# Hybrid attention and recurrence step: transposes of the decayed keys inside the value projection, four sample pages a run in both stages

## The chip, the cores and the metric

The kernel runs on one core of one Trainium2 chip, in one launch. The metric is device time in microseconds (us). TensorE (PE) does the matmuls, VectorE (DVE), ScalarE (ACT) and GpSimd (POOL) the elementwise work. SyncE (SP) issues almost all DMAs, in the order of its queue.

## The reference, cut to what matters

One decoder layer with width 2048, on 512 prompt tokens and 8 sample sequences of 8 tokens (576 columns together). All results are float32.

```python
z = rms_norm(x) @ w_in            # one combined projection, split into the parts below
# eight heads: sparse attention, top-k keys by an indexer; the samples read paged keys and values
att = sparse_attend(q, k_sel, v_sel, valid)
# four heads: gated linear attention (keys 128 wide, values 256 wide), in chunks
cum   = cumsum(log_a)
decay = exp(where(causal, cum_t - cum_s, -inf))
o     = (q * exp(cum)) @ S + einsum('tk,sk,tsk->ts', q, k, decay) @ v
S_new = exp(cum_last) * S + (k * exp(cum_last - cum)).T @ v
# output: gate both groups, join them, multiply by w_out, add x, normalise
```

The product `k * exp(cum_last - cum)` is the decayed key, `kD` in the kernel. `S_new` sums over tokens, so the kernel needs `kD` with tokens on the partitions: that is what the transposes of `kD` give.

## The kernel before

**Numbers.** Every large product is made of three matmuls on split operands (high times high, low weights times high, high times low). A weight tile is loaded by `wload`: SP brings 128x512 floats (256 KB) into `w_raw` (three slots), ACT casts the high part (`w_hi`, L181, five slots), DVE, or POOL late in the kernel, subtracts the low part (`w_lo`, L183, five slots). `gemm`/`kmm` is a projection with the tokens as columns: 288 columns a matmul, two for each product (L219, into `ps_g`). `vgroup` projects 512 columns of values with the tokens on partitions: sixteen steps of k, each with four row tiles of three matmuls (L608 to L610) and one tile for the samples with two (L604, L605, into `ps_v`), 512 columns each, one weight tile a step. At its end it scales the rows into `v_tok` (L638) and `v_smp` (L644) and stores them to a buffer in memory (`sv`, L640, L648).

**Stages.** Heads 0 to 3 of the attention come first, with the indexer; then heads 4 to 7; then, from about 640 us, the four heads h=0 to 3 of the recurrence; from about 1046 us the output projection (L1205 to L1210).

**Sample attention** is written once, in the generator `unit`, and is drawn step by step into the other work by `fill`: after each half of a `gemm` and each second step of a `vgroup` a rate is added to a sum, and each time the sum reaches one the next step of the unit is issued. A unit reads sixteen pages of keys or values (`kt`, `vt`; 1 MB each, four DMAs of 256 KB, `page_dma` L157, issued behind the page that was three earlier) into a ring tagged `kv`, and multiplies them in runs. `run` issues the first matmul of a list (L252) and ties the rest behind it at high priority (L255), so that nothing comes between. The scores go into `pS` (which L755 starts with a bias), then softmax, transposes (L787, L790), and the products with `vt` into `pOs`; ACT scales these into `ob` (L820), four transposes bring them into `pt` (L823), DVE gates them (L826). The units of the attention's second stage have four pages a run and a ring of five. Those of the recurrence's stage have two pages a run and a ring of four: sixteen runs.

**The recurrence, head by head.** `project` makes the log decay first (`log_decay`: two small matmuls into `ps_z` L896, ACT L897, L899 and L900 with a table load each, DVE L901 and the scan L903 into `cum`) and then the two projections of queries (`qT`, L923) and keys (`kT`). `decays` forms `ev_ec` (ACT L936) and `qE`; POOL writes the differences for `kD` (L943, L944), ACT takes the exponential (L945), POOL multiplies by the keys (L946). TensorE transposes `kD` (four times L949, once L953), ACT and DVE make `kDt`, `kDs` and `ks` of it (L951 to L963). Then eight levels of the triangular product within a chunk are set up (POOL L981 and L982, ACT L983, DVE L984 and L985, into `lv_d`) and multiplied in two runs (`pl`). A `yield` stands at the start of each of the two, and in the main loop the caller draws `decays` on from inside the value projection (h=0 and 1), the projections of head 3 (h=2) or the gates (h=3; L912 and L915). `recur` loads the values back (`vtok` L1049, `vSg` L1050) and does the chunks (L1066, L1067, L1072), the samples (L1082, L1095) and the transposes of the result (L1110, L1113 into `oT`, by ACT L1111 and L1114).

**Order.** A scheduler fixes each engine's order when the kernel is built, from the order of the code and from priorities; weights and runs have a higher priority (`WOFF`). On the chip each engine works its own list strictly in that order.

Of the kernel before, what the change touches and what calls it, by code (L numbers as in the profile page):

```python
# [20 lines left out]
P = 128  # L21
# [98 lines left out]
def build(tc, I, O):  # L120
# [4 lines left out]
    R0, R1, RF = 0.42, 0.65, 1.1  # L125
# [469 lines left out]
    def vgroup(g, step):  # L595
# [17 lines left out]
        for k in range(NK):  # L613
            w.append(wload(I["wv"][g, :, k : k + 1, :]))
            xs = ev.tile([P, P], F32R, name="xs", tag="xs", bufs=4)
            with tc.high_priority(offset=WOFF):
                po_.tensor_copy(xs[:, :TS], xh[k][:, TP:].bitcast(F32))
                po_.tensor_copy(xs[:, TS:], xl[k][:, TP:].bitcast(F32))
            xs2.append(xs)
            if k == 1:  # L620
                for i in (0, 1, 4, 2, 3):
                    for kk in (0, 1):
                        mms(i, kk)
            elif k == NK - 1:
                for i in range(5):
                    for kk in (NK - 2, NK - 1):
                        mms(i, kk)
            elif 1 < k < NK - 2:
                for i in range(5):
                    mms(i, k)  # L630
            if k % 2:
                fill()
            if k % 4 == 3:
                step(k // 4)
# [75 lines left out]
    def head(h, bg, n):  # L710
# [7 lines left out]
        if h == 0:  # L718
            for f in (head_q, head_k):
                qk1.append(f(1))  # L720
                pump(bg, n)
            vgroup(0, lambda q4: pump(bg, 2))
            filler[0] = None
            for _ in first:
                pass
            pa_s.close()
            px["p"], px["s"] = pool("pd1", 1)
            pump(bg, 3)
        Pi = head_scores(h, q, k)
        if h == 4:  # L730
            vgroup(1, lambda q4: None)
# [10 lines left out]
    def unit(un, w, hg, span):  # L742
# [10 lines left out]
        for half in range(2):  # L753
            S = pm.tile([P, 512], F32, name="pS", tag="pu", bufs=1)
            pe.matmul(S, lsel[half], biasS[:, :512], start=True, stop=False)  # L755
            for b0 in range(0, 4, span):
                mms = []
                for bb in range(b0, b0 + span):
                    kt = un.tile([P, 4, 512], F32, name="kt", tag="kv", bufs=max(span + 1, 4))
# [34 lines left out]
        for j0 in range(0, NPAGE, span):  # L794
            mms = []
            for j in range(j0, j0 + span):
                vt = un.tile([P, 4, 512], F32, name="vt", tag="kv", bufs=max(span + 1, 4))
# [34 lines left out]
    def chain(*gens):  # L832
        for g in gens:
            yield from g
# [15 lines left out]
    us = chain(unit(un, 0, 0, 4), unit(un, 1, 0, 4))  # L850
# [11 lines left out]
    us = chain(unit(un, 0, 1, 2), unit(un, 1, 1, 2))  # L862
# [67 lines left out]
    def decays(h, qT, kT, cum):  # L930
# [16 lines left out]
        pt = mm1("pt")  # L947
        for i in range(4):
            pe.transpose(pt[:, P * i : P * (i + 1)], kD[:, P * i : P * (i + 1)], ident)  # L949
        kDt = gl.tile([P, 4, P], F32, name="kDt")  # L950
        se.copy(kDt, pt.rearrange("p (i d) -> p i d", i=4))  # L951
        pt = mm1("pt")
        pe.transpose(pt[:, :P], kD[:, T - P : T], ident)  # L953
        kDs = ev.tile([TS, P], F32, name="kDs", tag="e1", bufs=2)
        se.copy(kDs, pt[TS:, :P])
        ks = [gl.tile([96, P], F32R, name=f"ks{w}") for w in range(2)]
        kept[h] = eL, qE, kDt, ks
        for w in range(2):
            r = slice(32 * w, 32 * w + 32)
            lo_r, hi_r = ((32, 0), (0, 32))[w]  # L960
            se.copy(ks[w][hi_r : hi_r + 32], kDs[r])
            se.copy(ks[w][64:96], kDs[r])
            ve.tensor_tensor(out=ks[w][lo_r : lo_r + 32], in0=kDs[r], in1=ks[w][r].bitcast(F32), op=ALU.subtract)  # L963
        Qd = bass.AP(tensor=Qb.tensor, offset=Qb.offset, ap=[Qb.ap[0], [64, 4], [32 + DT, 2], [1, DT]])
        po_.tensor_copy(Qd, qE[:, TP:T].rearrange("p (m e t) -> p m e t", e=2, t=DT))

# [5 lines left out]
        for B in (64, 32, 0, 16, 8, 4, 2, 1):  # L972
# [57 lines left out]
            if B in (16, 1):  # L1030
                yield
                run(*(m for level in reversed(mms) for m in level))
# [88 lines left out]
    for h in range(HB):  # L1121
# [7 lines left out]
        if h < 2:  # L1129
            vgroup(2 + h, lambda q4: next(d) if q4 in (0, 2) else None)  # L1130
# [210 lines left out]
```

## Time and profile before

| | us |
|---|---|
| median of 3 runs (lowest to highest) | 1256.31 (1256.11 to 1256.74) |
| the profiled execution | 1255.76 |
| its span, first to last instruction | 1254.0 |
| TensorE busy | 1218.5 (97%) |
| VectorE / ScalarE / GpSimd busy | 663.5 / 567.6 / 311.7 |

A row of an engine's timeline gives the start in us, the duration, the engine, the line, the operation with output and inputs, the shapes and how many there are; in brackets stands how long the engine was idle before it and what released it. Matmuls overlap, so the step from one start to the next is the cost of one, not its duration. The granted clock is the TensorE clock that the chip allowed, 1.00 being 2.4 GHz.

### The profile page before, as it was taken

Reading aid. Unit: us, or ns where it says so; the run is one execution under the profiler, and the core shown is the slowest. Engines: PE = TensorE matmul, PEld = TensorE weight load, DVE = VectorE, ACT = ScalarE, POOL = GpSimd, SP = SyncE. Lnnn points to the kernel's source line nnn. Section 1 sums busy time; section 2 is a strip of 40 time slices with the busy share of each in tenths; the row PEclk is TensorE's granted clock in tenths of the full one; section 3 lists DMA queues with packets and bytes.
Section 4 is the critical chain, followed back from the end, with each engine's and each line's share of the span. In section 5 each row is a group of like instructions: output and inputs, shape, how many; then the busy total and the mean of one; then the engine's idle time right before and its main releaser. Section 6 shows DMA issues by size and latency. Waiting matters only on the chain.

```text
span 1254.0 us, 23627 instructions
## 1 busy us (share of the span) xinstructions
PE 1218.5 (97%) x8695; PEld 1075.0 (86%) x8699; DVE 663.5 (53%) x1322; ACT 567.6 (45%) x1073; POOL 311.7 (25%) x483
## 2 busy tenths in 40 slices
PE   9999999999999999999999995999999899999996
PEld 8899987899997788888977784788899898888896
DVE  6678899699754214453446134424635656323243
ACT  7966664453443223443435234433636554223233
POOL 1224666445411101010106102300401402102021
PEclk9999999999999999999999997999999999999998
DMA  9652233423548496753576762856324247333335
GB/s 315 213 156 89 70 107 98 158 83 104 191 151 280 146 348 207 259 196 103 194 234 208 245 222 95 285 176 230 114 91 155 87 138 236 106 101 122 86 114 171
DMA packets 126885, 209.42 MB, mean 167 GB/s; under 512 B 14497, under 2 KB 37554, under 8 KB 126066
## 3 DMA queue, kind: packets, MB, share of 16 engines
q1 hardware_dynamic: 125682, 206.47, 50.0%
q8 instruction: 68, 1.11, 0.4%
q10 hardware_dynamic: 1088, 1.45, 0.4%
q14 instruction: 47, 0.39, 0.1%
HBM read 184.52 MB, written 23.22 MB: 166 GB/s over the span
## 4 chain that ended last, share of the span: by engine, by line
PE 85%; DVE 4%; ACT 3%; DMA 2%; POOL 2%; issue 2%; SPq 1%; DVEq 0%; ACTq 0%; POOLq 0%
PE ps_g L219 34%; PE acc L1207 5%; PE acc L1205 5%; PE acc L1206 5%; PE ps_g L227 5%; PE ps_g L608 5%; PE ps_g L609 5%; PE ps_g L610 5%; PE pS L255 1%; PE pOs L255 1%; PE ps_v L604 1%; PE acc L1210 1%; PE acc L1209 1%; PE ps_v L605 1%; PE pS L252 1%
## 5 line engine op out<-in xcount | busy, mean ns | idle before, releaser
L181 ACT CAST w_hi<-w_raw 128x512 fp32r<-128x512 f32 x316 | 193.4, 619 | 382.3 <-PE ps_g L219 138.6
L183 DVE TENSOR_TENSOR w_lo<-w_raw,w_hi 128x512 fp32r<-128x512 f32 x252 | 175.8, 704 | 331.4 <-ACT w_hi L181 313.2
L219 PE MATMUL ps_g<-xh,w_hi 128*128 128x288 f32 x1312 | 288.2, 299 | 0.7 <-ACT w_hi L198 0.7
L219 PE MATMUL ps_g<-xl,w_hi 128*128 128x288 f32 x1312 | 288.0, 298 | 0.0
L219 PE MATMUL ps_g<-xh,w_lo 128*128 128x288 f32 x1312 | 285.1, 297 | 0.0
L219 PEld LDWEIGHTS ps_g<-xh,w_hi 128*128 128x128 f32 x1312 | 212.9, 189 | 10.1 <-issue 5.9
L219 PEld LDWEIGHTS ps_g<-xh,w_lo 128*128 128x128 f32 x1312 | 212.8, 189 | 1.5 <-issue 0.4
L219 PEld LDWEIGHTS ps_g<-xl,w_hi 128*128 128x128 f32 x1312 | 213.0, 189 | 1.2 <-issue 0.6
L1206 PE MATMUL acc<-w_lo,mh 128*128 128x512 f32 (+1 forms) x320 | 110.7, 346 | 0.0
L1207 PE MATMUL acc<-w_hi,ml 128*128 128x512 f32 (+1 forms) x320 | 110.7, 346 | 0.0
L1205 PE MATMUL acc<-w_hi,mh 128*128 128x512 f32 (+1 forms) x320 | 110.3, 346 | 0.0
L608 PE MATMUL ps_g<-w_hi,xh 128*128 128x512 f32 x256 | 101.1, 395 | 0.0
L609 PE MATMUL ps_g<-w_lo,xh 128*128 128x512 f32 x256 | 100.0, 391 | 0.0
L610 PE MATMUL ps_g<-w_hi,xl 128*128 128x512 f32 x256 | 99.7, 390 | 0.0
L183 POOL TENSOR_TENSOR w_lo<-w_raw,w_hi 128x512 fp32r<-128x512 f32 x64 | 86.4, 1353 | 51.6 <-ACT w_hi L181 38.5
L1225 POOL TENSOR_TENSOR y<-y,nfb 128x512 f32<-128x512 f32 (+3 forms) x25 | 27.8, 1124 | 171.2 <-ACT yjk L1224 171.1
L1206 PEld LDWEIGHTS acc<-w_lo,mh 128*128 128x128 f32 x320 | 60.5, 189 | 7.5
L1205 PEld LDWEIGHTS acc<-w_hi,mh 128*128 128x128 f32 x320 | 60.4, 189 | 7.5
L1207 PEld LDWEIGHTS acc<-w_hi,ml 128*128 128x128 f32 x320 | 60.4, 189 | 7.5
L608 PEld LDWEIGHTS ps_g<-w_hi,xh 128*128 128x128 f32 x256 | 48.1, 188 | 14.0 <-issue 3.4
L610 PEld LDWEIGHTS ps_g<-w_hi,xl 128*128 128x128 f32 x256 | 48.1, 188 | 10.2
L609 PEld LDWEIGHTS ps_g<-w_lo,xh 128*128 128x128 f32 x256 | 48.1, 188 | 9.7
(338 smaller groups left out, 1983.0 us busy)
## 6 DMA issues: line engine op xcount, KB each, us to landing
w_raw<-in_w SPq DMA_DIRECT2D x188, 256.0 KB, 2.9
kt<-in_ck SPq DMA_DIRECT2D x128, 256.0 KB, 4.8
vt<-in_cv SPq DMA_DIRECT2D x128, 256.0 KB, 5.4
w_raw<-in_wv SPq DMA_DIRECT2D x64, 256.0 KB, 3.0
w_raw<-in_wo SPq DMA_DIRECT2D x64, 256.0 KB, 2.8
xr<-in_xT SPq DMA_DIRECT2D x16, 288.0 KB, 4.4
xt<-in_xp SPq DMA_DIRECT2D x4, 1024.0 KB, 8.1
sv<-v_tok SPq DMA_DIRECT2D x16, 256.0 KB, 3.7
```

Source lines behind the costliest of these rows:

```text
L181: se.copy(hi, raw)
L183: lo_eng[0].tensor_tensor(out=lo, in0=raw, in1=hi.bitcast(F32), op=ALU.subtract)
L219: pe.matmul(ps[:, j, :HT], wt, xt[:, j * HT : (j + 1) * HT], start=(k == 0 and n == 0), stop=(k == NK - 1 and n == 2),)
L227: pe.matmul(ps[:, 0, :TQ], wt[:, c], xt[:, P:T], start=(k == 0 and n == 0), stop=(k == NK - 1 and n == 2))
L255: f()
L608: pe.matmul(accs[i], xh[k][:, c], wh, start=a, stop=False)
L609: pe.matmul(accs[i], xh[k][:, c], wl, start=False, stop=False)
L610: pe.matmul(accs[i], xl[k][:, c], wh, start=False, stop=b)
L1205: pe.matmul(acc, mh[k][:, tsl], wh, start=(k == 0), stop=False)
L1206: pe.matmul(acc, mh[k][:, tsl], wl, start=False, stop=False)
L1207: pe.matmul(acc, ml[k][:, tsl], wh, start=False, stop=(k == NK - 1))
L1225: po_.tensor_tensor(out=yc, in0=yc, in1=nfb[:r, cs], op=ALU.mult)
```

## The change

1. The filler's rate in the recurrence's stage (`R1`) goes from 0.65 to 0.4. The units of this stage take four pages a run, with a ring of five slots (`unit`'s last argument is now the ring).
2. The transposes of `kD`, with `kDt`, `kDs` and `ks`, become a function `rows_of_k`, called after the first `yield` of `decays`, directly ahead of the first run of levels. The copy into `Qb` stays where it was.
3. `vgroup` calls `step(k)` at every k. For h=0 and 1 the main loop draws `decays` on at k=5 and 11; it did so at k=3 and 11. The two other calls of `vgroup` do what they did.

```diff
-    R0, R1, RF = 0.42, 0.65, 1.1
+    R0, R1, RF = 0.42, 0.4, 1.1
...
             if k % 2:
                 fill()
-            if k % 4 == 3:
-                step(k // 4)
+            step(k)
...
-    def unit(un, w, hg, span):
+    def unit(un, w, hg, pages):
+        span = 4
...
-                    kt = un.tile([P, 4, 512], F32, name="kt", tag="kv", bufs=max(span + 1, 4))
+                    kt = un.tile([P, 4, 512], F32, name="kt", tag="kv", bufs=pages)
...
-    us = chain(unit(un, 0, 1, 2), unit(un, 1, 1, 2))
+    us = chain(unit(un, 0, 1, 4), unit(un, 1, 1, 4))
...
         po_.tensor_tensor(out=kD, in0=kT, in1=kD, op=ALU.mult)
-        pt = mm1("pt")
-        for i in range(4):
-            pe.transpose(pt[:, P * i : P * (i + 1)], kD[:, P * i : P * (i + 1)], ident)
-        kDt = gl.tile([P, 4, P], F32, name="kDt")
-        se.copy(kDt, pt.rearrange("p (i d) -> p i d", i=4))
...
         po_.tensor_copy(Qd, qE[:, TP:T].rearrange("p (m e t) -> p m e t", e=2, t=DT))
+
+        def rows_of_k():
+            pt = mm1("pt")
+            for i in range(4):
+                pe.transpose(pt[:, P * i : P * (i + 1)], kD[:, P * i : P * (i + 1)], ident)
+            kDt = gl.tile([P, 4, P], F32, name="kDt")
+            se.copy(kDt, pt.rearrange("p (i d) -> p i d", i=4))
...
             if B in (16, 1):
                 yield
+                if B == 16:
+                    rows_of_k()
                 run(*(m for level in reversed(mms) for m in level))
...
         if h < 2:
-            vgroup(2 + h, lambda q4: next(d) if q4 in (0, 2) else None)
+            vgroup(2 + h, lambda k: next(d) if k in (5, 11) else None)
```

In the changed file the later lines have other numbers: L949 is L953 there, L953 is L957, L983 is L985, and from the levels' runs on every line is four higher (L1067 is L1071).

**TensorE at h=1.** The second head's transposes of `kD`, before. `oT`'s transposes end, then come the log decay's products and the sample result:

```order
L1113 MATMUL pt<-c_ident,osb 128x128
L896 MATMUL ps_z<-abS,wgS 128x288 x2
L823 MATMUL pt<-c_ident,ob 128x128 x4
L755 LDWEIGHTS selw
L755 MATMUL pS<-biasS,selw 128x512
L949 MATMUL pt<-c_ident,kD 128x128 x4
L953 MATMUL pt<-c_ident,kD 128x128
L604 MATMUL ps_v<-w_hi,xs 128x512
L605 MATMUL ps_v<-w_lo,xs 128x512
```

The transposes L949 stand directly behind L823 and the bias product L755, ahead of the whole value projection (L604 on). After the change the same place reads:

```order
L896 MATMUL ps_z<-abS,wgS 128x288
L755 LDWEIGHTS selw
L755 MATMUL pS<-biasS,selw 128x512
L823 MATMUL pt<-c_ident,ob 128x128 x4
L604 MATMUL ps_v<-w_hi,xs 128x512
L605 MATMUL ps_v<-w_lo,xs 128x512
```

The value projection now follows L823 at once. Its matmuls come between L823 and the transposes, 74 of them, and then:

```order
L609 MATMUL ps_g<-w_lo,xh 128x512
L953 MATMUL pt<-c_ident,kD 128x128 x4
L252 MATMUL pS<-kt,qz 32x512
L255 MATMUL pS<-kt,qz 32x512 x15
L957 MATMUL pt<-c_ident,kD 128x128
L252 MATMUL pl<-lv_d 32x16
L255 MATMUL pl<-lv_d 32x16 x15
```

The transposes (now L953 and L957) stand around a run of four pages (fifteen matmuls behind the first, instead of seven), ahead of the first run of levels (`pl`).

**ACT at h=1**, between the second half of `oT` and the exponential of the decay, before:

```order
L1111 ACTIVATE oT<-pt,gnorm 128x512
L1114 ACTIVATE oT<-pt,gnorm 128x64
L897 ACTIVATE ld_e<-ps_z,bgate 128x288 x2
L899 ACT_TABLE_LOAD
L899 ACTIVATE ld_e<-ld_e 128x576
L900 ACT_TABLE_LOAD
L900 ACTIVATE ld_e<-ld_e 128x576
L820 ACTIVATE ob<-pOs,mxs 128x512
L936 ACT_TABLE_LOAD
L936 ACTIVATE ev_ec<-cum 128x576
```

and after:

```order
L1115 ACTIVATE oT<-pt,gnorm 128x512
L820 ACTIVATE ob<-pOs,mxs 128x512
L1118 ACTIVATE oT<-pt,gnorm 128x64
L897 ACTIVATE ld_e<-ps_z,bgate 128x288 x2
L899 ACT_TABLE_LOAD
L899 ACTIVATE ld_e<-ld_e 128x576
L181 CAST w_hi<-w_raw 128x512
L900 ACT_TABLE_LOAD
L900 ACTIVATE ld_e<-ld_e 128x576
L181 CAST w_hi<-w_raw 128x512 x3
L936 ACT_TABLE_LOAD
L936 ACTIVATE ev_ec<-cum 128x576
```

`ob` (L820) moved from behind the table loads of L899 and L900 to ahead of L897, and weight casts (L181) moved in between the steps of the log decay.

**TensorE at h=0, behind the first value projection of this stage**, where the last pages of the first unit are multiplied. Before:

```order
L252 MATMUL pOs<-vt,prT 32x512
L255 MATMUL pOs<-vt,prT 32x512 x7
L255 MATMUL pOs<-vaS,prT 32x512 x4
L1067 MATMUL pO<-vtok,att 128x256
L1072 MATMUL pUg<-vtok,kDt 128x256
```

Two runs and 96 projection matmuls stand before this place and behind the value projection; the product that reads `vtok` comes directly after. After the change:

```order
L252 MATMUL pOs<-vt,prT 32x512
L255 MATMUL pOs<-vt,prT 32x512 x15
L255 MATMUL pOs<-vaS,prT 32x512 x4
L219 MATMUL ps_g<-xh,w_hi 128x288 x2
L219 MATMUL ps_g<-xh,w_lo 128x288 x2
L219 MATMUL ps_g<-xl,w_hi 128x288 x2
```

The one run of four pages stands directly behind the value projection, and 60 projection matmuls (L219) lie between it and the product that reads `vtok` (now L1071).

**SP at the same place**: the load of the stored values (`vtok`, `vSg`) among pages (`kt`) and weights. Before:

```order
L157 ISA
L157 DMA kt<-in_ck 128x512
L178 DMA w_raw<-in_wv 128x512
L1049 DMA vtok<-sv_475 128x4x256
L648 DMA sv_475<-v_smp 64x512
L178 DMA w_raw<-in_wv 128x512 x2
L1050 DMA vSg<-sv_475 64x256
```

and after:

```order
L647 DMA sv_475<-v_smp 64x512
L157 ISA
L157 DMA kt<-in_ck 128x512
L152 TENSOR_LOAD ptab
L157 ISA
L157 DMA kt<-in_ck 128x512
L1053 DMA vtok<-sv_475 128x4x256
L157 ISA
L157 DMA kt<-in_ck 128x512
L157 ISA
L157 DMA kt<-in_ck 128x512
L1054 DMA vSg<-sv_475 64x256
```

The store of the samples' values (`sv<-v_smp`) moved ahead of `vtok`, and `vtok` and `vSg` stand closer together, with page pieces between instead of weights. Between the last store of `v_tok` and `vtok` there are four page pieces, six before.

## Rows read from the trace of the kernel before

**Rows 1.** The page, part 1: busy time of the engines.
```profile
PE 1218.5 (97%) x8695; PEld 1075.0 (86%) x8699; DVE 663.5 (53%) x1322; ACT 567.6 (45%) x1073; POOL 311.7 (25%) x483
```
**Rows 2.** Waits of TensorE, the two longest: us in total, times, longest us.
```profile
PE pt L949 <- POOL kD L946: 15.1, 3, 9.0
PE pt L823 <- ACT ob L820: 5.2, 1, 5.2
```
**Rows 3.** Timeline of TensorE, h=1.
```profile
767.50 0.40 PE L896 MATMUL ps_z<-abS,wgS 128*128 128x288 f32 x1 [0.18 <-ACT oT L1111]
773.05 1.12 PE L823 MATMUL pt<-c_ident,ob 128*128 128x128 f32 x4 [5.16 <-ACT ob L820]
783.21 1.12 PE L949 MATMUL pt<-c_ident,kD 128*128 128x128 f32 x4 [9.04 <-POOL kD L946]
```
**Rows 4.** Timeline of TensorE, h=2 and h=3.
```profile
901.32 0.66 PE L949 MATMUL pt<-c_ident,kD 128*128 128x128 f32 x4 [1.99 <-POOL kD L946]
...
971.93 0.42 PE L219 MATMUL ps_g<-xh,w_lo 128*128 128x288 f32 x2
...
972.73 0.43 PE L219 MATMUL ps_g<-xh,w_lo 128*128 128x288 f32 x2
...
977.32 0.90 PE L949 MATMUL pt<-c_ident,kD 128*128 128x128 f32 x3 [4.03 <-POOL kD L946]
```
**Rows 5.** Stretches: length, busy us (instructions) by engine, granted clock, DMA share, GB/s.
```profile
768.00:787.00 19.00, 4.91 (x17) 3.94 (x18) 8.86 (x15) 12.01 (x21) 11.31 (x22) 0.55 0.19 66
...
900.00:907.00 7.00, 5.68 (x124) 5.34 (x125) 5.76 (x13) 4.73 (x15) 6.03 (x8) 0.76 0.26 80
```
**Rows 6.** Timeline of ACT, h=1.
```profile
767.52 0.91 ACT L897 ACTIVATE ld_e<-ps_z,bgate 128x288 f32<-128x288 f32 x2
...
772.33 0.67 ACT L820 ACTIVATE ob<-pOs,mxs 128x512 f32<-128x512 f32 x1
```
**Rows 7.** Timeline of POOL, h=1.
```profile
781.59 1.57 POOL L946 TENSOR_TENSOR kD<-kT,kD 128x576 f32<-128x576 f32 x1
```
**Rows 8.** Timeline of TensorE, end of the value projection at h=0.
```profile
710.65 0.39 PE L608 MATMUL ps_g<-w_hi,xh 128*128 128x512 f32 x1
...
712.69 0.39 PE L605 MATMUL ps_v<-w_lo,xs 128*128 128x512 f32 x1
```
**Rows 9.** Timelines of DVE (h=2) and ACT (h=3).
```profile
890.28 0.75 DVE L923 SCALAR_TENSOR_TENSOR qT<-ps_g,rstd 128x576 f32<-128x576 f32 x1
...
960.14 1.28 ACT L912 ACT_TABLE_LOAD   x1
961.44 0.69 ACT L912 ACTIVATE og<-og 128x576 f32<-128x576 f32 x1
```
**Rows 10.** Timeline of TensorE around a run of four pages and one of two.
```profile
394.50 0.62 PE L252 MATMUL pS<-kt,qz 128*32 128x512 f32 x1
...
398.07 0.33 PE L676 MATMUL pq<-kh,qh 128*128 128x128 f32 x1
...
654.86 0.62 PE L252 MATMUL pS<-kt,qz 128*32 128x512 f32 x1
...
656.72 0.50 PE L608 MATMUL ps_g<-w_hi,xh 128*128 128x512 f32 x1
657.05 0.39 PE L609 MATMUL ps_g<-w_lo,xh 128*128 128x512 f32 x1
```
**Rows 11.** A stretch between two runs of four pages, columns as in Rows 5.
```profile
437.00:450.00 13.00, 13.00 (x60) 10.44 (x56) 1.39 (x2) 2.84 (x5) 0.84 (x5) 1.00 1.00 335
```
**Rows 12.** SP and TensorE at h=0; landing times of vtok, then of all sv transfers.
```profile
723.20 0.39 SPq L1049 DMA_DIRECT2D vtok<-sv  x1
...
730.55 0.70 PE L1067 MATMUL pO<-vtok,att 128*128 128x256 f32 x2
...
DMA to landing us min/median/max: 6.7/6.7/6.7
...
DMA to landing us min/median/max: 2.1/4.6/6.7
```

More of the change, by code (lines that the diff above doesn't have):

```diff
@@ L721, in head @@
                 pump(bg, n)
-            vgroup(0, lambda q4: pump(bg, 2))
+            vgroup(0, lambda k: pump(bg, 2) if k % 4 == 3 else None)
             filler[0] = None
@@ L730, in head @@
         if h == 4:
-            vgroup(1, lambda q4: None)
+            vgroup(1, lambda k: None)
         v = head_v(h)
@@ L796, in unit @@
             for j in range(j0, j0 + span):
-                vt = un.tile([P, 4, 512], F32, name="vt", tag="kv", bufs=max(span + 1, 4))
+                vt = un.tile([P, 4, 512], F32, name="vt", tag="kv", bufs=pages)
                 page_dma(
@@ L849, in build @@
     un, un_s = pool("unit", 1, side="right")
-    us = chain(unit(un, 0, 0, 4), unit(un, 1, 0, 4))
+    us = chain(unit(un, 0, 0, 5), unit(un, 1, 0, 5))
     filler[:] = [us, R0, 0.0]
@@ L946, in decays @@
         po_.tensor_tensor(out=kD, in0=kT, in1=kD, op=ALU.mult)
-        pt = mm1("pt")
-        for i in range(4):
-            pe.transpose(pt[:, P * i : P * (i + 1)], kD[:, P * i : P * (i + 1)], ident)
-        kDt = gl.tile([P, 4, P], F32, name="kDt")
-        se.copy(kDt, pt.rearrange("p (i d) -> p i d", i=4))
[L952 to L963, printed above, removed]
         Qd = bass.AP(tensor=Qb.tensor, offset=Qb.offset, ap=[Qb.ap[0], [64, 4], [32 + DT, 2], [1, DT]])
         po_.tensor_copy(Qd, qE[:, TP:T].rearrange("p (m e t) -> p m e t", e=2, t=DT))
+        def rows_of_k():
[4 more added lines that the diff above has]
+            se.copy(kDt, pt.rearrange("p (i d) -> p i d", i=4))
+            pt = mm1("pt")
+            pe.transpose(pt[:, :P], kD[:, T - P : T], ident)
+            kDs = ev.tile([TS, P], F32, name="kDs", tag="e1", bufs=2)
+            se.copy(kDs, pt[TS:, :P])
+            ks = [gl.tile([96, P], F32R, name=f"ks{w}") for w in range(2)]
+            kept[h] = eL, qE, kDt, ks
+            for w in range(2):
+                r = slice(32 * w, 32 * w + 32)
+                lo_r, hi_r = ((32, 0), (0, 32))[w]
+                se.copy(ks[w][hi_r : hi_r + 32], kDs[r])
+                se.copy(ks[w][64:96], kDs[r])
+                ve.tensor_tensor(out=ks[w][lo_r : lo_r + 32], in0=kDs[r], in1=ks[w][r].bitcast(F32), op=ALU.subtract)
         attD = gl.tile([P, 5, 32], F32, name="attD")
```

## The prediction

> **What bounds the kernel now.** I read the list of TensorE's waits first, then TensorE's rows around each wait, then the rows of the engine that it waited for. TensorE is busy for 97% of the span [rows 1], so a change pays only where TensorE stands still, runs at the lower clock, or does its own work faster. The span is 1254.0 us and TensorE's 1218.5 us leave 35.5 us of idle time. The list shows where the long pieces are: three waits of the first transposes of the decayed keys (L949) on the POOL product kD, 15.1 us together, and one wait of 5.2 us of the transposes of a sample result (L823) on ACT's ob [rows 2]. All four lie in the recurrence's stage, which the change edits.
>
> The two largest stand one behind the other at head h=1 [rows 3]. The small product ps_z ends at 767.90. TensorE then waits 5.16 us for ob, does 1.1 us of transposes, and waits 9.04 us for kD. At h=2 and h=3 the same transposes wait 1.99 and 4.03 us [rows 4]. After such a stand the granted clock is at its lower level, 1.2 of 2.4 GHz: 0.55 on average from 768 to 787, 0.76 from 900 to 907 [rows 5]. If the records know only full and half clock, 0.55 over 19 us is 17.1 us at half, about 769.1 to 786.2, and 0.76 over 7 us is 3.4 us.
>
> **Why the stand at h=1 is so long.** kD comes out of a chain that begins at ps_z: ACT L897, two table loads with two activations, DVE's scan (cum), then POOL, which does two differences for kD and six for the levels before the product L946 at 781.59, 1.57 us long [rows 6, 7]. The product ends at 783.16, 15.3 us after ps_z. In the old order TensorE has nothing ahead of L949 in that time, because the transposes stand in front of the projection of values. ob is ready to be made much earlier, but ACT has it queued behind both table loads, at 772.33 [rows 6].
>
> **Term 1, h=1: -16.2 us.** In the new order the bias product (L755), L823 and 74 matmuls of the value projection stand between ps_z and the transposes. One such matmul is issued every 0.227 us (nine steps in 2.04 us) [rows 8], so 74 are 16.8 us. With 0.3 for L755 and 0.6 for L823 the transposes come 17.8 us after ps_z. The chain gets longer: ACT now has weight casts of 0.62 us within it (one ahead of L900, three ahead of L936, one ahead of L945), of which the three lie beside DVE's subtraction and scan. I put kD at 15.3 + 0.62 + 0.62 = 16.5 us, which leaves 1.2 us. ob stands ahead of L897 on ACT, behind one short activation of oT, so its wait goes. What goes is 5.16 + 9.04 = 14.2 us of stand, and the lower clock behind it: 3.0 us of work up to 786.2 at half clock cost 1.5 us, the four L823 transposes at 1.12 instead of some 0.6 us another 0.5. Sum 16.2. Lost if the chain is late: up to 2 us, which is the three casts in full. What covers the chain are the 74 matmuls, and these need their weights: if ACT casts them too late, the cover is gone (first rival).
>
> **Term 2, h=2 and h=3: -2.3 us.** Here the transposes are held back a little too, but the order puts no more work ahead of them: 105 matmuls of the projection with 288 columns and one L823 group at h=2, 119 at h=3. What moves is the chain. At h=2 DVE no longer does qT (0.75 us) ahead of the scan [rows 9]; 1.99 becomes about 1.2, gain 0.8. At h=3 the table load and gate activation of L912 (960.14 to 962.13, 1.99 us [rows 9]) go from ahead of L900 to behind L936, where POOL's own queue hides them; four projection matmuls less stand in front, 0.5 us at 0.133 us each (six steps in 0.80 us [rows 4]). 4.03 becomes about 2.5, gain 1.5. Bounds: nothing, and both stands gone with the low clock behind them (1.99 + 1.6 and 4.03 + 1.7, the 3.4 us at half clock being worth 1.7).
>
> The two rows of L912 show a table load of 1.28 us and the activation 0.02 us behind it. The Trainium skill, "ScalarE: Activation LUTs", section "What ACT_TABLE_LOAD costs", says that a switch costs about 2.66 us, since a drain of 1.38 us follows the load; these rows do not show that drain. By the page's price the move at h=3 would bring 1.4 us more and the time would be about 1236.6 us.
>
> **Term 3, pages: -2.2 us.** Eight runs of four pages replace sixteen of two. A run of four takes 3.57 us to the start of the next matmul (394.50 to 398.07), one of two 1.86 (654.86 to 656.72), so two of two take 0.15 more. Each run also costs at its exit: the next matmul takes 0.33 us instead of 0.23, 0.10 more, and some 0.09 at its entry by the same kind of gap [rows 10]. That is 0.34 for each of eight merged pairs, at most 2.7; pairs that already stood back to back save only 0.15 (three or so). I take 2.2, bounds 0 and 2.7. This needs the pages to be there. A run now frees four of five slots, so three pages must be loaded before the next run: twelve pieces of 0.262 MB, and four weight pieces, 4.2 MB. The shortest distances in the new order are 50 and 43 value matmuls with a level run between: 12.9 and 13.1 us, 323 GB/s. In the attention stage, with the same ring of five and runs of four, 13 us between runs pass at 335 GB/s with TensorE busy for all 13.00 us [rows 11]. So I put the wait at 0, with a bound of 1 us each.
>
> **Term 4, a new wait at h=0: +2.4 us.** This one comes from the old filler leaving. Before, 96 projection matmuls and two page runs stand between the end of the first value projection (712.9) and the first recurrence product L1067 at 730.55 [rows 8, 12]. Now one run and 60 matmuls do: 3.7 + 0.4 + 60 x 0.133 = 12.1, so TensorE is there after some 12.5 us instead of 17.6. L1067 reads vtok, which SP loads back from what the projection stored. SP issued it at 723.20, 10.3 us after the projection, and it took 6.7 us to land, at 729.9: it was in time by 0.6 us [rows 12]. In the new order SP still has all stores of the values ahead of it. Issued at the same distance it lands after 17.0 us, 4.5 too late; with the shortest landing of the same transfers, 2.1 us, it is in time; with their median, 4.6 us, it is 2.4 us late. I take the median, since four page pieces instead of six stand between the last store of values and vtok. Bounds 0 and 5.1 (the whole distance lost), with 1.6 of lower clock on top.
>
> **The sum.** -16.2 - 2.3 - 2.2 + 2.4 = -18.3. Made against the profiled execution of 1255.76 us (its span of 1254.0 and 1.8 around it) that is 1237.5. The median of the runs shown is 0.55 higher, so the forecast is **1238 us**. The bounds: all the good ends give -16.2 - 9.3 - 2.7 = -28.2, 1228; all the bad ones -14.2 + 0 + 0 + 6.7 + 2 = -5.5, 1251.
>
> **The rivals.**
> *The cover at h=1 is not there (the change does not do what it says).* The value matmuls need a cast on ACT each 3.2 us (14 matmuls), and ACT is in the decay chain with three table loads. If TensorE waits for casts, or kD is later still, the 9.04 us and the low clock stay and only ob's 5.16 goes: -5.2 - 2.3 - 2.2 + 2.4 = -7.3, 1249. Against it: the order has casts inside the chain, and table loads are 1.28 us each against a ring of five weights. Chance 0.08.
> *vtok's wait takes the removed one's place in full:* 5.1 + 1.6 instead of 2.4, the rest as forecast: 1242. For it: vtok's own landing of 6.7 us. Chance 0.17.
> *The stand at h=3 goes altogether, and vtok is in time:* -16.2 - 0.8 - (4.03 + 1.7) - 2.2 = -24.9, 1231. For it: the chain there needs to gain only 2.5 us more, and ACT's order was loosened just there. Against it: POOL still does a gate's product ahead of kD. Chance 0.10.
> *Slower: runs of four wait for their pages.* SP works its queue in order and the ring holds one page ahead, so TensorE stands at each short distance. Four of the seven distances are short by the count of matmuls in them: 17.1, 12.9, 13.1 and 18.6 us. If the 4.2 MB take 13 us, as in the attention stage, nothing happens; if they take 20, the waits are 2.9 + 7.1 + 6.9 + 1.4 = 18.3, with some 1.6 of low clock at each 24.7, and the sum is +6.4: 1263. It decides from about 19 us. Against it: rows of the same pattern pass at 335 GB/s [rows 11]; for it: they pass with the DMA engines at 1.00. Chance 0.05.
>
> **How the numbers follow.** Forecast 0.60, in 1234 to 1241; rivals 0.08, 0.17, 0.10, 0.05. The range 1230 to 1249 takes in all but the page rival and the ends of two others, some 0.13. About 0.2% (2.5 us) is what a measurement of this kernel can tell from no change. Faster by more than that: 0.93; within it, where several bad ends and a mild page wait meet, 0.03; slower 0.04.
>
> **What would show it.** In the list of waits L949 (L953 in the new numbering) should fall from 15.1 to about 4 us, with nothing at h=1, and L823 should leave it; the granted clock at h=1 should stay at 1.00. A wait of the product that reads vtok, on a DMA, of about 2 us would show term 4. Rows of page runs should have no wait, and be 3.57 us long. The prediction is wrong if a page run waits, if matmuls of the value projection wait for casts, or if L953 still waits at h=1.

## The result and the profile after

The changed kernel takes 1243.05 us in the median of six runs (1241.47 to 1249.52), the kernel before beside it 1256.21 (1255.06 to 1259.39): a ratio of 0.9901, 95% interval 0.9877 to 0.9925. A second set of runs on another occasion (experiment 8 below) gave 0.9926 (0.9911 to 0.9941). So it is faster by 9 to 12 us, inside the range of 1230 to 1249, and short of the forecast of 1238 by 5 us, by the second set by 8.

One statement on the change, ahead of the prediction, is wrong, and a term of the prediction rests on it. The last argument of `unit` is the ring: it is 5 in the attention's second stage and **4** in the recurrence's stage. I read the 4 there as pages a run and put the ring at five. With runs of four and a ring of four, no page is loaded ahead: the pages of a run can come in only as the run before it gives its slots free (in the row of SP in experiment 4 the first piece is issued 1.45 us after the run before it has begun).

The profiled execution took 1241.47 us, 14.3 less than the 1255.76 before; it is the fastest of the six, and the medians are 13.2 apart. The page's first lines and its list of TensorE's waits, longest first (us in total, times, longest; to be held against [rows 1, 2]):

```profile
PE 1214.6 (98%) x8699; PEld 1074.7 (87%) x8699; DVE 666.1 (54%) x1322; ACT 568.1 (46%) x1074; POOL 313.1 (25%) x483
```
```profile
PE pt L953 <- POOL kD L946: 5.0, 3, 2.0
PE pO L1071 <- DMA vtok<-sv: 2.5, 1, 2.5
...
PE pS L252 <- DMA kt<-in_ck: 1.1, 1, 1.1
PE pOs L252 <- DMA vt<-in_cv: 1.0, 1, 1.0
...
PE pl L255 <- issue: 0.9, 1, 0.9
PE pl L252 <- DVE lv_d L987: 0.9, 1, 0.9
PE pl L252 <- ACT kDt L955: 0.5, 1, 0.5
PE ps_g L608 <- ACT w_hi L181: 0.5, 1, 0.5
```

The wait for ob is gone, the waits for kD fell from 15.1 to 5.0 us, and new ones stand in the list: vtok, and two waits for pages that I had not counted. TensorE's timeline at the places of [rows 3, 4] and at the new waits:

```profile
712.23 0.59 PE L252 MATMUL pOs<-vt,prT 128*32 128x512 f32 x1 [0.98 <-DMA vt<-in_cv]
...
727.45 0.67 PE L1071 MATMUL pO<-vtok,att 128*128 128x256 f32 x2 [2.52 <-DMA vtok<-sv]
...
767.79 0.29 PE L896 MATMUL ps_z<-abS,wgS 128*128 128x288 f32 x1
...
768.16 0.60 PE L823 MATMUL pt<-c_ident,ob 128*128 128x128 f32 x4
...
787.84 0.66 PE L953 MATMUL pt<-c_ident,kD 128*128 128x128 f32 x4 [1.39 <-POOL kD L946]
...
806.29 0.59 PE L252 MATMUL pS<-kt,qz 128*32 128x512 f32 x1 [1.07 <-DMA kt<-in_ck]
...
883.95 0.66 PE L953 MATMUL pt<-c_ident,kD 128*128 128x128 f32 x4 [1.53 <-POOL kD L946]
...
885.26 0.18 PE L252 MATMUL pl<-lv_d 128*32 128x16 f32 x1 [0.55 <-ACT kDt L955]
...
958.09 0.97 PE L953 MATMUL pt<-c_ident,kD 128*128 128x128 f32 x4 [2.02 <-POOL kD L946]
```

At h=1 L823 follows the log decay's products within 0.4 us, and 9.04 us in front of the transposes became 1.39. The stretches that answer to [rows 5] (length, busy us by engine, granted clock, DMA share, GB/s) show that the lower clock is gone at h=1 and at h=2, where 1.53 us of stand are left, and that it stayed at h=3, where 2.02 are left:

```profile
768.00:788.00 20.00, 18.13 (x81) 14.34 (x81) 14.20 (x21) 13.94 (x20) 14.14 (x27) 1.00 0.45 140
...
884.00:892.00 8.00, 7.46 (x147) 7.15 (x148) 7.80 (x16) 6.10 (x17) 6.87 (x8) 1.00 0.19 68
...
958.00:966.00 8.00, 7.91 (x140) 7.41 (x141) 7.83 (x15) 6.08 (x17) 7.85 (x10) 0.79 0.19 68
```

### The profile page after: what moved, and what is told of

Read it like the earlier page. It is cut to its first block, busy times and chain, and to the rows that moved or that the text cites. A ratio compares the mean times of both kernels' runs of the same rounds, so it can differ in the third digit from the quotient of the medians.

```text
span 1239.7 us, 23613 instructions
## 1 busy us (share of the span) xinstructions
PE 1214.6 (98%) x8699; PEld 1074.7 (87%) x8699; DVE 666.1 (54%) x1322; ACT 568.1 (46%) x1074; POOL 313.1 (25%) x483
## 3 DMA queue, kind: packets, MB, share of 16 engines
q10 hardware_dynamic: 1088, 1.45, 0.4%
## 4 chain that ended last, share of the span: by engine, by line
PE 83%; DVE 5%; DMA 3%; POOL 3%; ACT 3%; issue 2%; SPq 0%; POOLq 0%; ACTq 0%; DVEq 0%
PE ps_g L219 34%; PE acc L1211 5%; PE acc L1210 5%; PE acc L1209 5%; PE ps_g L227 5%; PE ps_g L608 4%; PE ps_g L610 4%; PE ps_g L609 4%; PE pS L255 2%; PE pOs L255 2%; PE acc L1214 1%; PE acc L1213 1%; PE ps_v L604 1%; PE ps_v L605 1%; DVE wk L497 1%
## 5 line engine op out<-in xcount | busy, mean ns | idle before, releaser
L181 ACT CAST w_hi<-w_raw 128x512 fp32r<-128x512 f32 x316 | 193.1, 619 | 363.0 <-PE ps_g L219 130.3
L183 DVE TENSOR_TENSOR w_lo<-w_raw,w_hi 128x512 fp32r<-128x512 f32 x252 | 181.7, 727 | 307.2 <-ACT w_hi L181 287.4
L219 PE MATMUL ps_g<-xl,w_hi 128*128 128x288 f32 x1312 | 288.5, 298 | 0.0
L219 PE MATMUL ps_g<-xh,w_hi 128*128 128x288 f32 x1312 | 287.2, 298 | 0.2 <-ACT w_hi L198 0.2
L219 PE MATMUL ps_g<-xh,w_lo 128*128 128x288 f32 x1312 | 285.5, 296 | 0.0
L219 PEld LDWEIGHTS ps_g<-xh,w_hi 128*128 128x128 f32 x1312 | 212.5, 188 | 8.9 <-issue 4.2
L219 PEld LDWEIGHTS ps_g<-xl,w_hi 128*128 128x128 f32 x1312 | 213.0, 189 | 1.5 <-issue 0.8
L219 PEld LDWEIGHTS ps_g<-xh,w_lo 128*128 128x128 f32 x1312 | 212.7, 188 | 1.1 <-DVE w_lo L199 0.2
L608 PEld LDWEIGHTS ps_g<-w_hi,xh 128*128 128x128 f32 x256 | 48.0, 188 | 13.2 <-issue 1.7
L617 POOL CAST xs<-xh 128x64 fp32r<-128x64 f32 x64 | 19.4, 304 | 146.9 <-PE ps_v L605 141.7
```

The costliest lines, as they stand in the source:

```text
L181: se.copy(hi, raw)
L183: lo_eng[0].tensor_tensor(out=lo, in0=raw, in1=hi.bitcast(F32), op=ALU.subtract)
L219: pe.matmul(ps[:, j, :HT], wt, xt[:, j * HT : (j + 1) * HT], start=(k == 0 and n == 0), stop=(k == NK - 1 and n == 2),)
L608: pe.matmul(accs[i], xh[k][:, c], wh, start=a, stop=False)
```

## The experiments

The first two ask which part pays, the next ones what made each term smaller than forecast, the last ones whether a better version follows.

**1. The pages alone.** The kernel before, with

```diff
-    R0, R1, RF = 0.42, 0.65, 1.1
+    R0, R1, RF = 0.42, 0.4, 1.1
...
-    us = chain(unit(un, 0, 1, 2), unit(un, 1, 1, 2))
+    us = chain(unit(un, 0, 1, 4), unit(un, 1, 1, 4))
```

Two more lines, not shown, set the ring, which stays at four slots there.

> Only the sample pages change: four pages a run, the ring of four slots that the recurrence's stage has in both kernels, rate 0.4. The transposes stay at their old place ahead of the value projection. Theory (the transposes' cover is what pays): TensorE still stands some 14 us for ob and kD at h=1, the merged runs give back about 2 us, the waits for pages (2 us) and for vtok (2.5 us) take them again: 1254 to 1258 us, ratio 0.998 to 1.002. Rival (the pages are what pays): 1246 us or less. The list of waits should show L949 with 13 us or more.

Measured: 1256.36 us, ratio 0.9998 (0.9987 to 1.0009): no gain. Its list of waits, first line:

```profile
PE pt L949 <- POOL kD L946: 17.8, 3, 14.6
```

The 5.2 us for ob are gone in this kernel too, because the units end sooner and ACT makes ob ahead of the log decay. But the wait for kD is 14.6 us instead of 9.0: without work of its own in front of it, TensorE just arrives earlier at the same end of the chain, which here too comes 15.2 us behind ps_z (15.3 before). What the prediction counted as two stands, 5.16 and 9.04, is one chain with ob's transposes in the middle.

**2. The transposes alone.** The changed kernel with the old pages:

```diff
-    R0, R1, RF = 0.42, 0.4, 1.1
+    R0, R1, RF = 0.42, 0.65, 1.1
...
-        span = 4
+        pages = max(span + 1, 4)
...
```

The units of the recurrence's stage get runs of two and a ring of four, as before.

> Only the transposes move (and the steps to k=5 and 11); pages in runs of two as before. Theory: the stand at h=1 falls from 14.2 to 4 us or less, with the low clock behind it, and no wait for vtok and for pages appears, since the old filler (96 projection matmuls and two runs) stands there again: 1240 to 1245 us, about as fast as the whole change. Rival (both parts are needed): 1249 us or more.

Measured: 1248.45 us, ratio 0.9944 (0.9927 to 0.9961): 7 us, about half. The time lies between the theory's bound (1245) and the rival's (1249), nearer to the rival's, and the trace speaks for the rival. The list has no wait for kD at h=1 and none for vtok, but

```profile
PE pt L953 <- POOL kD L946: 6.0, 2, 4.0
PE pt L823 <- ACT ob L820: 5.2, 1, 5.2
PE pS L252 <- DMA kt<-in_ck: 1.5, 1, 1.5
```

The wait for ob stays, since ob is still behind ACT's two table loads. The wait for pages, at 801.68, is one that the expectation had excluded: runs of two do not rule it out. So the parts are worth 0 and 7 us alone and 9 to 12 together. The pages' part pays by where it puts ob, and only when the transposes have moved.

**3. ob from another ring, with the transposes moved and the old pages.** In the code ob shares the ring `e0` with oT, and in the changed kernel ACT's row of ob waits for a store of oT to release it. Experiment 2, with one edit more:

```diff
-        ob = ev.tile([P, 512], F32, name="ob", tag="e0", bufs=2)
+        ob = ev.tile([P, 512], F32, name="ob", tag="e1", bufs=2)
```

> The kernel with the transposes moved and the old pages (runs of two), and besides ob taken from the ring e1 instead of e0, which it shared with oT; by that ACT makes ob ahead of the log decay, as in the changed kernel. Theory: the 5.2 us for ob (left when the transposes alone were moved, 1248.5 us) go with the low clock behind them, and none of the waits for pages and vtok that the longer runs brought appear: 1241 to 1243 us, as fast as the whole change or a little faster. Rival (ob's wait only hides a wait for kD behind it): the stand moves to the transposes of kD and the time stays at 1246 to 1248.

Measured: 1244.81 us, ratio 0.9911 (0.9897 to 0.9925), 3.6 us less than experiment 2 and level with the whole change. Its waits:

```profile
PE pt L953 <- POOL kD L946: 7.6, 3, 4.0
```

Nothing for ob, pages or vtok; 1.6 us of the 5.2 came back as a wait for kD at h=1, and the 1.5 us for pages of experiment 2 went as well. A gain of the same size is thus to be had without longer page runs: on balance, what the longer runs brought was the place of ob.

**4. Half the bytes a page.**

```diff
-    kt = un.tile([P, 4, 512], F32, name="kt", tag="kv", bufs=pages)
+    kt = un.tile([P, 4 - 2 * hg, 512], F32, name="kt", tag="kv", bufs=pages)
```

`vt` is edited likewise, and each page has two DMAs.

> The changed kernel, but in the recurrence's stage each sample page has half its bytes (two DMAs of 256 KB, not four, in slots of half the size; the matmuls read each half twice, so shapes and counts stay, and the attention of four heads' samples works on half the keys). Theory: the two waits for pages (2.0 us together) are the DMA engines, full while four new pages come in between two runs; with half the bytes both go and 2 to 3 us are gained: 1239 to 1241 us. Rival (the waits are the order of SP's queue or the release of the slots, not the bytes): they stay at 1 us each and the time stays at 1242 to 1244.

Measured: 1240.34 us, ratio 0.9868 (0.9852 to 0.9885). Both waits for pages are gone, and vtok's fell to 0.8 us. The stretches in front of the two waiting runs in the changed kernel, then the one in front of the first of them in this kernel:

```profile
699.00:712.00 13.00, 12.25 (x127) 9.88 (x118) 2.54 (x9) 2.51 (x4) 3.81 (x15) 1.00 0.92 311
...
793.00:806.00 13.00, 12.22 (x258) 10.01 (x248) 10.12 (x24) 7.07 (x19) 8.11 (x14) 1.00 1.01 340
```
```profile
699.00:713.00 14.00, 14.00 (x208) 10.89 (x201) 2.54 (x9) 2.60 (x5) 2.99 (x11) 1.00 0.69 227
```

The pages set these waits, and in the changed kernel the DMA engines are at 0.92 and 1.01 of their time while they come in. But the edit halves the number of DMAs with the bytes, and SP's row in the changed kernel shows a second limit at the same place, behind the run at 788.42:

```profile
789.87 10.88 SPq L157 DMA_DIRECT2D kt<-in_ck  x16
```

SP needs 0.68 us to issue one piece, 10.9 for the sixteen of a run; the last is issued at 800.75 and the run starts at 806.29. Full engines are not needed for that length: in experiment 7 the first four pieces start 0.53 us apart (796.01, 796.54, 797.08, 797.60), right behind two microseconds in which the DMA engines move nothing. The bytes count too: at this place a piece takes 5.3 us from its issue to its landing in the changed kernel and 3.6 here (medians). Which of the two, issue or bytes, a single change would free is left open. The executions of this kernel lie between 1238 and 1241 us, those of the changed kernel between 1240 and 1249; that the pages make the difference fits, but no trace of an execution of the changed kernel above 1243 us was taken (experiment 8), so it is not shown.

**5. vtok without its detour.**

```diff
-        sy.dma_start(vtok, sv[:TP].rearrange("(i p) c -> p i c", p=P))
+        sy.dma_start(vtok, spill_v[0][:TP, DV * (h % 2) : DV * (h % 2) + DV].rearrange("(i p) c -> p i c", p=P))
```

> The changed kernel, but vtok is loaded from the values of an earlier group that were stored hundreds of us before, so that the load has to wait for no store of this stage (the recurrence then works on other values; same sizes, same queue). Theory: the 2.5 us wait of L1071 on vtok is the way of the values out to memory and back, so it goes, and 2 to 3 us with it: 1240 to 1241 us. Rival (the DMA engines are full at that point and any load there would be late): a wait of 1.5 us or more stays.

Measured: 1242.29 us, ratio 0.9892 (0.9877 to 0.9907), not to be told from the changed kernel. The edit did more than take out one load. Without the stores to wait for, the scheduler moved the first products that read vtok ahead of the run of pages (to 712.51; the run starts at 713.47), and the log decay of h=1 came 13 us earlier (its second product at 754.53 instead of 767.79). The wait for vtok went, as the theory says, the waits for pages left the list too, and another took their place:

```profile
731.50 0.70 PE L1070 MATMUL pO<-Sst,qE 128*128 128x256 f32 x2 [3.14 <-DVE Sst L1081]
```
```profile
730.51 0.42 DVE L1060 TENSOR_TENSOR vs<-vSg,vs 32x256 fp32r<-32x256 f32 x1 [5.77 <-ACT vs L1059]
730.96 0.48 DVE L1081 SCALAR_TENSOR_TENSOR Sst<-Sst,eL,pUg 128x256 f32<-128x256 f32 x1
```

The first row is TensorE's, the others are VectorE's. The state product waits for Sst, and on VectorE Sst stands behind the split of vSg, which is the same way out to memory and back (issued at 726.0, landed 4.1 us later). In this order, then, the detour holds the place up through another tile. What taking the one load off would give in an unchanged order is not shown.

**6. GpSimd beside an idle VectorE.** In the changed kernel the chain from the end of ps_z to kD took 19.7 us (768.08 to 787.78) at h=1, 15.3 before. Two of the differences that GpSimd makes ahead of kD, and the product:

```profile
777.94 1.13 POOL L983 TENSOR_TENSOR lv_d<-cum 128x256 f32<-128x256 f32 x1
779.03 1.06 POOL L984 TENSOR_TENSOR lv_d<-cum 128x256 f32<-128x256 f32 x1
...
786.39 1.39 POOL L946 TENSOR_TENSOR kD<-kT,kD 128x576 f32<-128x576 f32 x1
```

The kernel before did the same two in 0.62 and 0.61 us. VectorE's rows there and here differ by the low weights that it now makes at the same time. So these were left out there, by an argument of `wload` that hands in a low tile:

```diff
...
-            w.append(wload(I["wv"][g, :, k : k + 1, :]))
+            w.append(wload(I["wv"][g, :, k : k + 1, :], lo_of=w[0][1] if g == 3 and k else None))
```

> The changed kernel, but the value projection at h=1 reuses its first low weight tile for all sixteen steps, so VectorE makes no w_lo there (fifteen subtractions of 0.7 us and more left out; the values of two heads lose their low part). Theory: GpSimd's steps on the way to kD take about twice their time while VectorE works beside them (1.1 instead of 0.6 us for one level difference), and that made the chain from ps_z to kD 19.7 instead of 16.5 us; without the subtractions the differences take 0.6 us again, kD is ready 2 to 4 us earlier, and L953 does not wait at h=1: 1240 to 1242 us. Rival (the longer chain comes from ACT's casts and GpSimd's own casts alone): the differences stay at 1.1 us and L953 still waits.

Measured: 1241.69 us, ratio 0.9885 (0.9869 to 0.9901). The lines of this kernel are two higher:

```profile
777.87 0.62 POOL L985 TENSOR_TENSOR lv_d<-cum 128x256 f32<-128x256 f32 x1
778.46 1.13 POOL L986 TENSOR_TENSOR lv_d<-cum 128x256 f32<-128x256 f32 x1
779.54 0.63 POOL L985 TENSOR_TENSOR lv_d<-cum 128x256 f32<-128x256 f32 x1
...
784.40 1.42 POOL L948 TENSOR_TENSOR kD<-kT,kD 128x576 f32<-128x576 f32 x1
```
```profile
777.87 1.24 DVE L943 TENSOR_TENSOR qE<-qT,ev_ec 128x576 f32<-128x576 f32 x1 [1.40 <-ACT ev_ec L938]
```
```profile
787.67 0.60 PE L955 MATMUL pt<-c_ident,kD 128*128 128x128 f32 x4
```

Five of the six differences take what they took before (the last two, 0.84 and 0.80, stood beside VectorE's products for the levels there too). The one at 1.13 stands beside the product qE; the one ahead of it, which starts together with qE, takes 0.62, and it is qE that takes 1.24. So two such instructions side by side do not always slow GpSimd's; one of them is late. kD is ready at 785.82, 16.6 us after ps_z (769.25), 3.1 us sooner than in the changed kernel, and the transposes do not wait. The theory holds. The Trainium skill, "GPSIMD Engine Reference", section "1. Specifications", says that GpSimd shares its SBUF interfaces with VectorE and contends with VectorE instructions that have two inputs in SBUF; the rows agree, and where GpSimd is the one held up they give the price here, 1.06 to 1.13 us against 0.62. In the time the gain (1.4 us of wait) is no larger than what separates two sets of runs of the changed kernel.

**7. kD's last product on VectorE.**

```diff
-        po_.tensor_tensor(out=kD, in0=kT, in1=kD, op=ALU.mult)
+        ve.tensor_tensor(out=kD, in0=kT, in1=kD, op=ALU.mult)
```

> The changed kernel with the last product of kD (L946) on VectorE instead of GpSimd, nothing else edited. Theory: GpSimd's queue, with six level differences, four small copies and the casts of xs ahead of that product, is what makes kD late in the changed kernel (19.7 us after ps_z at h=1), so the three waits for kD (5.0 us) go nearly all, and 2 to 4 us are gained: 1238 to 1241 us. Rival (the chain up to the exponential L945 is what is late, or the first run of levels then waits for lv_d instead): the waits move from the transposes to the levels' run and the time stays at 1242 to 1244 us.

Measured: 1251.78 us, ratio 0.996 (0.9945 to 0.9974): by the ratios slower than the changed kernel by 4 to 7 us (0.9926 and 0.9901), which neither side expected. The list of waits:

```profile
PE pS L252 <- DMA kt<-in_ck: 4.8, 1, 4.8
PE pt L953 <- DVE kD L946: 3.9, 2, 2.9
PE pl L252 <- DVE lv_d L987: 3.1, 3, 1.6
PE pOs L252 <- DMA vt<-in_cv: 2.1, 1, 2.1
```

kD's wait went at h=1, as the theory says. At h=2 it fell to 1.02 us and at h=3 it grew to 2.85, and the levels' run waits 1.31 and 1.60 us there, as the rival says. Most of what made the kernel slower is a third thing, 6.9 us of waits for pages instead of 2.1. SP's queue ahead of the longer one:

```profile
785.62 4.93 SPq L178 DMA_DIRECT2D w_raw<-in_wv  x3
795.13 0.33 SPq L178 DMA_DIRECT2D w_raw<-in_w  x1
796.01 10.56 SPq L157 DMA_DIRECT2D kt<-in_ck  x16
```

What SP waited for from 790 to 796, and the DMA engines ahead of the pieces and while they come in:

```profile
SPq L178 <- DVE w_lo L183: 4.5, 1, 4.5
```
```profile
794.00:796.00 2.00, 2.00 (x110) 1.83 (x102) 1.29 (x4) 0.80 (x2) 0.41 (x1) 1.00 0.00 0
796.00:811.70 15.70, 10.90 (x195) 8.88 (x185) 7.45 (x20) 5.26 (x12) 7.16 (x19) 1.00 0.95 319
```

The run in front starts at 791.02 (it waits 1.5 us for qz). From 790.55 to 795.13 SP issues nothing: a weight load stands next in its queue and waits for VectorE's subtraction of an earlier weight, which ends at 795.09; it stands behind two products for the levels that begin only at 793.74. The sixteen pieces behind it begin 5.0 us after the start of the run instead of 1.45 (788.42 to 789.87 in the changed kernel). These 3.5 us are nearly all of what the wait of the next run grew by (1.07 to 4.80). So the prediction's page rival is real in this form: the ring holds no page ahead, and whatever holds up SP's queue goes straight into TensorE's wait.

**8. The changed kernel again, and kD's product ahead of the differences.** The changed kernel twice more, unedited:

> The changed kernel once more, unedited, as a control beside the next run on the same chip: 1241 to 1246 us, ratio 0.988 to 0.993. If it comes out near 0.988, the gain of steps at k=3 and 11 seen before (0.9883) is not to be told from the changed kernel; if near 0.992, it is.

> The changed kernel, unedited, one more look. Its executions lie between 1240 and 1249 us, wider than those of the kernel with half pages (1238 to 1241), and only the two at 1240 and 1241 us have a trace so far. If this one falls at 1245 us or more, the list of waits should show where: longer waits for pages and vtok (theory: the DMA engines, full at the short distances, vary from run to run), or other places (rival).

Measured: 1246.46 us (1240.06 to 1248.72), ratio 0.9926 (0.9911 to 0.9941); and one execution of 1242.62. The traces, of executions at 1240 and 1243 us, show the waits of the first one, vtok at 2.1 and 2.4 us and the two for pages at 1.3 us or less, so where the executions above 1243 us lose more was not seen. In the three traces of the changed kernel the wait for pages at h=0 grows with the time: none in the list at 1240.06 us, 0.98 at 1241.47, 1.27 at 1242.62. But pages are not all of the spread: at the log decay of h=0, near the start of the changed stage, the slowest of the three is already 1.6 us behind the fastest (644.04 and 642.42). On the same chip as the control ran a kernel in which GpSimd's differences are issued behind the product of kD (and the steps are drawn at k=3 and 11):

```diff
...
+                with tc.issue_after(km):
                    po_.tensor_tensor(out=dv[:, :, 1, :], in0=cv[:, :, 1, :], in1=ref, op=ALU.subtract)
                    po_.tensor_tensor(out=dv[:, :, 0, :], in0=ref, in1=cv[:, :, 0, :], op=ALU.subtract)
```

> Meant to beat both: steps at k=3 and 11, and GpSimd makes the product of kD ahead of the level differences (these are issued behind it), so kD no longer stands behind six differences. Theory: kD is ready some 5 us earlier at h=1, 2 and 3, and the three waits of L953 (5.0 us) go; the level differences come 1.6 to 2.5 us later, so the first run of levels at h=2 and h=3 waits instead, by about what is saved there. Only the 1.4 us at h=1 and perhaps the low clock at h=3 (1.7 us) are gained: 1239 to 1242 us. Rival (POOL then idles while it waits for ACT's exponential, and everything behind comes later): 1244 us or more.

Measured: 1245.65 us, ratio 0.9913 (0.9898 to 0.9929), the same as the control. The waits say why:

```profile
PE pl L252 <- DVE lv_d L989: 6.0, 3, 2.7
...
PE pt L954 <- POOL kD L946: 1.8, 2, 1.0
```

5.0 us of waiting for kD became 1.8 for kD and 6.0 for the levels, 0.9 before. kD and the levels come out of one queue on GpSimd, and both are wanted at one place; here their order chose the name of the wait and not the time.

**9. The place of the steps.**

```diff
-            vgroup(2 + h, lambda k: next(d) if k in (5, 11) else None)
+            vgroup(2 + h, lambda k: next(d) if k in (3, 11) else None)
```

> The changed kernel with the steps of decays drawn at k=3 and 11, as before, instead of 5 and 11. It moves the transposes of h=0 forward by 28 value matmuls (6.3 us); at h=1 nothing moves. Theory: at h=0 the transposes then wait for kD by 0 to 3 us, and the time is 1243 to 1247 us. Rival (kD of h=0 is ready early enough anyway): no wait at h=0, 1242 to 1244.

> The steps at k=3 and 11 once more, as a candidate that beats both kernels (0.9883 at first, with four runs; the changed kernel 0.9901 and 0.9926). If it is faster by what its trace showed (no wait for pages ahead of the first value products, 0.6 us instead of 1.1 at the other short distance): 1241 to 1244 us, ratio 0.988 to 0.990. If the first result was chance: 0.991 to 0.993.

Measured: 1241.92 us, ratio 0.9883 (0.9867 to 0.9898), and 1241.35, 0.9892 (0.9875 to 0.9910). No wait for kD at h=0, so the later step was not needed: the rival of the first run was right. The waits for pages are 0.6 and 0.3 us in all, instead of 2.1. It beats the kernel before. That it beats the changed kernel is not shown: both its intervals overlap that of the first set (0.9877 to 0.9925), and only the second set (0.9911 to 0.9941) lies above them.

## Why the prediction was right in kind and short in size

The forecast came out in the right direction and inside its range. Of the signs that the prediction named for being right, ob's wait is gone, the clock at h=1 stays at 1.00, and vtok's wait is there; L953 fell to 5.0 us in all, not to about 4. The three signs that it named for being wrong all came too, each small: two runs wait for pages (0.98 and 1.07 us), a matmul of the value projection waits for a cast (0.47), and L953 still waits at h=1 (1.39). The terms can be read one by one. Forecast, then what the profiled execution gives, in us; in its column the lower clock (2.0 at h=1, 1.6 at h=2) and the entries and exits of the runs (1.3) are the prediction's own prices and not measured. That the sum comes out near the difference of the executions is no check of them:

| | forecast | from the trace after |
|---|---|---|
| h=1 | -16.2 | -14.3 |
| h=2 and h=3 | -2.3 | about -1.8 |
| pages | -2.2 | about +0.5 |
| vtok | +2.4 | +2.5 |
| ahead of the stage | 0 | -1.0 |
| sum | -18.3 | -14.1 (the executions: -14.3) |

The -1.0 ahead of the stage is a difference between two executions; nothing was edited there.

**h=1** was right in mechanism: 74 matmuls cover the chain, ob's wait goes, the granted clock stays at 1.00. Its size was off by 1.39 us of wait for kD and 0.47 for a weight cast, inside the bound of 2. The step that failed is kD at 16.5 us. It was ready 19.7 us after ps_z. I added two casts and nothing for the work that VectorE and GpSimd now do for the value projection during the chain: the scan ends 1.0 us later (7.7 instead of 6.7 after ps_z), and GpSimd needs 11.8 instead of 8.4 us from its first difference to kD, of which the slow differences make 1.7 and two casts of xs 1.0. Experiment 6 takes VectorE's part away and gets 16.6. The cover was itself a load on the chain. That the two stands were one chain (experiment 1) did not change this term, since the whole of it was covered.

**h=2 and h=3.** The waits became 1.53 and 2.02, forecast 1.2 and 2.5. I had not foreseen that the levels' run, now directly behind the transposes, waits for the copy that frees their buffer (0.55) and later for its own levels (0.88 at h=3; 0.89 at h=2 that the profile gives to no one). The new waits, 2.3 us, take back nearly all of the 2.5 that the old ones gave. What is left in the table is the lower clock at h=2, which is gone, some 1.6 us by the prediction's own price. That the term comes out near its forecast is therefore in good part luck, and the price looks too high here. In the second trace of experiment 9, whose edit leaves h=2 and h=3 alone, the clock fell at h=2 (the stretch below), behind the same 1.53 us, and stayed at 1.00 at h=3 (957 to 965). From the transposes of h=2 to those of h=3 this trace takes 74.9 us; the three traces of the changed kernel, with the full clock at h=2, take 74.1, 74.4 and 74.1, and the first trace of experiment 9, also with the full clock, 74.7. So the lower clock cost 0.2 to 0.8 us there. At h=3 it cost nothing; the rows with it (the changed kernel) and without it (experiment 9):

```profile
884.00:892.00 8.00, 7.91 (x140) 7.77 (x141) 7.80 (x16) 6.06 (x17) 6.55 (x8) 0.79 0.19 68
```
```profile
970.81 0.18 PE L252 MATMUL pl<-lv_d 128*32 128x16 f32 x1 [0.88 <-DVE lv_d L987]
```
```profile
957.66 0.66 PE L953 MATMUL pt<-c_ident,kD 128*128 128x128 f32 x4 [2.02 <-POOL kD L946]
...
970.43 0.18 PE L252 MATMUL pl<-lv_d 128*32 128x16 f32 x1 [2.32 <-DVE lv_d L987]
```

From the transposes to the second run of levels it is 12.7 us with the lower clock (958.09 to 970.81) and 12.8 without. At full clock TensorE is there sooner and waits for the levels instead.

As for the table loads: the changed kernel's rows, too, show an activation 0.02 us behind a load.

```profile
768.64 1.28 ACT L899 ACT_TABLE_LOAD   x1
769.94 0.69 ACT L899 ACTIVATE ld_e<-ld_e 128x576 f32<-128x576 f32 x1
```

The price of 2.66 us a switch that the Trainium skill gives ("ScalarE: Activation LUTs", "What ACT_TABLE_LOAD costs") does not appear in these rows.

**Pages** is the term that failed, and the ring was misread. With a ring of four, 16 pieces and some four weights, 5.2 MB, must pass in a short distance, not 12 and four, 4.2 MB, and the row that I leaned on [rows 11] has a ring of five. I had also priced the bytes only, and not SP's 0.68 us for each piece. The two waits of 0.98 and 1.07 us stand where the prediction named the shortest distances, and at its bound of 1 us each. No run here has five slots in this stage, so how much of them the fifth would have saved stays open. The merge gave less, too: the eight runs take 30.5 us to the next matmul, the sixteen took 30.8, where 0.15 for each of eight pairs would be 1.2. That leaves the entries and exits, some 1.3 us by the price of [rows 10] (0.19 for each of seven pairs; one stood back to back before), which no run measures alone.

**vtok** was right to 0.1 us, partly because two errors cancel. SP issued it at 721.85, 10.6 us after the end of the projection (711.25; forecast 10.3), and it took 5.5 us to land (forecast 4.6); TensorE came 1.2 us later than forecast, 0.98 of it by the wait for pages in between. Experiment 5, in an order of its own, shows the samples' values waiting on the same detour.

**The rivals.** The cover held but for the 0.47 and 1.39 us, so the first fell. The page rival was worth 2 us here and 7 in experiment 7. The sum of the two parts' own gains, 0 and 7, shows what the prediction did not say: the parts depend on each other.

## What to carry to other kernels

Work that is put in front of a late operand as cover brings its own casts, subtractions and loads onto the engines that make the operand; add them to the chain before judging the cover. Two waits that stand behind each other on one engine may be one chain: removing the first alone gives nothing (experiment 1). With runs as long as the ring nothing is loaded ahead, and the time to issue and land a whole run has to fit between any two runs (experiments 4 and 7).

## What the hardware showed that I had not expected

A 128x256 float32 difference on GpSimd took 0.62 us beside an idle VectorE and 1.06 to 1.13 us where VectorE's float32 products and subtractions with two inputs in SBUF ran beside it; where it started together with such a product it took 0.62 us, and the product 1.24 (experiment 6). On SP the issue of one 256 KB page piece took 0.66 to 0.68 us on average, and 0.53 right behind a stretch in which the DMA engines moved nothing, so a run of sixteen pieces costs 10.6 to 10.9 us of SP's queue before the last of them has been issued. The lower clock at h=3, 0.79 on average over 8 us, cost nothing, since the next wait took it up.
